# State update of a chunked recurrence: decay of both directions on GpSimd, one addition per head on VectorE

## Chip, cores and metric

One core of a Trainium2 chip runs the kernel. The metric is the device time of one launch in microseconds (us), as the median of the runs shown. Inputs and outputs are float32. TensorE is the matmul engine (PE), VectorE is DVE, ScalarE is ACT, GpSimd is POOL, SyncE is SP, which issues most of the DMAs.

## What is computed

One layer of a hybrid network on 1024 tokens of 2048 features and 256 context tokens: an adaptive layer norm, the input projection `w_in`, three branches (an S5 state space, a pooling branch and an RWKV recurrence), the output projection `w_out`, and a layer norm. The change concerns the RWKV branch: 16 heads of 64, two directions, started from the final states of the context. Its reference, token by token:

```python
def _rwkv_scan(s0, r, w, k, v, kk, kka, reverse, want_out):
    def step(s, inp):
        w_t, k_t, v_t, kk_t, kka_t = inp[:5]
        s_kk = jnp.einsum('bhvk,bhk->bhv', s, kk_t)
        s = (s * w_t[:, :, None, :] - s_kk[..., None] * kka_t[:, :, None, :]
             + v_t[..., None] * k_t[:, :, None, :])
        if want_out:
            return s, jnp.einsum('bhvk,bhk->bhv', s, inp[5])
        return s, None
```

The state `s` of a head is 64x64; it fades by `w_t` per feature and gains outer products.

## The kernel before

The first half (phases A and B, up to about 1700 us) does the layer norm, the input projection and the S5 and pooling branches. Phase C runs the recurrence in chunks of 64 tokens. Two heads make a pair, so there are eight pairs; both directions of a pair go side by side. A pair has four quarters of four chunks, 16 steps in all, and before them four steps over the context (`prefixes`), which only build the starting state. That makes 128 steps and 32 prefix steps.

A step (`c_first`, `c_second`, `c_third`) is a chain. On TensorE, L2009 multiplies the state of each direction with the queries, and L2014 adds the chunk's own part. ScalarE copies the result (`rhs`, L2018). L2024 applies the solved 64x64 system, ScalarE copies (`uv`, L2028), L2037 forms what the state gains, in the bank `b_u`, and L2043 completes the outputs, which ScalarE copies out (`outs`, L2056). Then VectorE updates the state (L2050; L2119 in the prefix): one `scalar_tensor_tensor` per direction and head, state times the chunk's decay `el`, plus the gain from PSUM. In the last step of a pair there is no update. The state lies in `ping`, a 128x128 tile per direction with the two heads as blocks on the diagonal.

Beside the chain other jobs run. `seg_job` loads keys, spreads them into tiles with zero blocks (`spread`, L236 and L234), multiplies (L1745) and masks (L1750). `solve` inverts the small triangles on VectorE (`tmp` and `nn`, L1880 and L1882). `jit_jobs` scale the queries on GpSimd (`qt`, L1843). `finish` normalizes a pair's outputs, in part on GpSimd (`gof`, `gvn`, `gs`), and stores them to `y`. `out_first` takes 12 of the 16 row blocks of the projection `w_out` ahead of time: it loads pieces, gates and splits them into a high and a low half (L240, L234, L236), multiplies three times (L2434 to L2436) and adds to a partial sum in DRAM (`ofev`, L2451 and L2453, then `part`).

The order on every engine is written by a planner, `Pace`. It keeps a clock of its own for each engine; a job yields `need(engine, cost, due times)`. After each third of a step, `fill` lets the planner put other jobs' work into the queues until TensorE's planned time reaches the time when the chain can go on:

```python
        def fill(ch, third=False):
            t = max(ch.t_s[0], ch.t_s[1] - 0.22, ch.t_o) if third else ch.t
            P.offer(max(P.free["pe"] + QUOTA, t + SLACK))
```

So the price that a step's code names decides how much other work stands between two steps. Engines then run their queues strictly in this order.

When the last pair's last quarter begins, the pool of keys (`st`) is closed and `Late.begin` takes its room for the last four blocks of `w_out` (`dwraw`, `dgate`, `dwhi`, `dwlo`, L2503 to L2526). Phase D multiplies these with the last outputs (L2623 to L2625), adds the partial sums (`pre`, loaded from `part`, L2641) and does the final layer norm. `dacc` has four banks, each freed by its addition L2641.

## Time and profile before

| what | value |
|---|---|
| median of 3 runs | 3001.09 us (2996.73 to 3008.69) |
| the profiled execution | 3004.46 us, span 3002.7 us |
| mean granted TensorE clock | 0.928 of full speed |
| PE busy | 2703.1 us (90%) |
| DVE busy | 2017.4 us (67%) |
| ACT busy | 1053.1 us (35%) |
| POOL busy | 1058.8 us (35%) |
| phase C, from the first keys to the last step | about 1700 to 2845 us |
| state update, L2050 and L2119 | 608 instructions, 134.2 + 35.8 us |

The profile tells of one execution. Shares over the whole span mix stages: the input projection until 1650 us is a dense run of large matmuls, while phase C is what the change touches. So a reader goes from the table of stages to the waits in a stage, and from there to single steps in order of time. An instruction's idle time in front of it, with what ended it, stands in square brackets in the timeline.

### The profile page before, as it was taken

Reading aid. Unit: us, or ns where it says so; the run is one execution under the profiler, and the core shown is the slowest. Engines: PE = TensorE matmul, PEld = TensorE weight load, DVE = VectorE, ACT = ScalarE, POOL = GpSimd, SP = SyncE. Lnnn points to the kernel's source line nnn. Section 1 sums busy time; section 2 is a strip of 40 time slices with the busy share of each in tenths; the row PEclk is TensorE's granted clock in tenths of the full one; section 3 lists DMA queues with packets and bytes.
Section 4 is the critical chain, followed back from the end, with each engine's and each line's share of the span. In section 5 each row is a group of like instructions: output and inputs, shape, how many; then the busy total and the mean of one; then the engine's idle time right before and its main releaser. Section 6 shows DMA issues by size and latency. Waiting matters only on the chain. (4 is left out here: it accounts for less than half of the span.)

```text
span 3002.7 us, 56320 instructions
## 1 busy us (share of the span) xinstructions
PE 2703.1 (90%) x20080; PEld 2194.4 (73%) x20080; DVE 2017.4 (67%) x4463; ACT 1053.1 (35%) x2668; POOL 1058.8 (35%) x1432
## 2 busy tenths in 40 slices
PE   7989999999999999999899669988988889898776
PEld 2258878888888887777777467877878778787555
DVE  5548136655666657888888375768778777876458
ACT  1321224444444443222122223343434334443313
POOL 0104003333343334223552133454444434444316
PEclk9989999999999999999999778999979889898688
DMA  7834646667666665555344665676675756564354
GB/s 272 262 109 139 152 123 169 168 170 190 175 171 179 168 174 156 158 161 165 106 116 124 198 192 145 189 186 166 166 190 169 203 146 188 149 182 123 83 199 158
DMA packets 698673, 498.48 MB, mean 166 GB/s; under 512 B 347182, under 2 KB 624406, under 8 KB 695574
## 3 DMA queue, kind: packets, MB, share of 16 engines
q1 hardware_dynamic: 672632, 449.52, 53.8%
q0 software_dynamic: 6912, 24.12, 2.9%
q10 hardware_dynamic: 18848, 21.24, 2.0%
q8 instruction: 159, 2.61, 0.4%
q14 instruction: 122, 1.00, 0.1%
HBM read 339.64 MB, written 155.07 MB: 165 GB/s over the span
## 5 line engine op out<-in xcount | busy, mean ns | idle before, releaser
L300 PE MATMUL pm<-hi,whi 128*128 128x512 f32 x1600 | 512.2, 402 | 4.4 <-ACT whi L300 4.3
L300 PE MATMUL pm<-hi,wlo 128*128 128x512 f32 x1600 | 509.4, 400 | 3.8 <-DVE wlo L300 3.8
L300 PE MATMUL pm<-lo,whi 128*128 128x512 f32 x1600 | 510.0, 400 | 0.0
L300 DVE TENSOR_TENSOR wlo<-wraw,whi 128x256 fp32r<-128x256 f32 x400 | 227.8, 576 | 317.6 <-ACT whi L300 297.8
L300 PEld LDWEIGHTS pm<-hi,whi 128*128 128x128 f32 x1600 | 275.3, 190 | 58.3 <-ACT whi L300 6.2
L300 PEld LDWEIGHTS pm<-hi,wlo 128*128 128x128 f32 x1600 | 275.5, 190 | 55.6 <-DVE wlo L300 5.8
L300 PEld LDWEIGHTS pm<-lo,whi 128*128 128x128 f32 x1600 | 274.5, 190 | 51.1 <-issue 2.2
L300 ACT ACTIVATE whi<-wraw 128x256 fp32r<-128x256 f32 x400 | 160.8, 415 | 415.6 <-DMA wraw<-in_w_in 241.3
L2434 PE MATMUL ofacc<-ofhi,ofyh 128*128 128x256 f32 x768 | 252.1, 328 | 25.9 <-DVE ofev L2451 16.0
L240 POOL TENSOR_TENSOR oflo<-ofw,ofhi 128x256 fp32r<-128x256 f32 x158 | 119.9, 759 | 342.0 <-ACT ofhi L234 226.2
L2435 PE MATMUL ofacc<-ofhi,ofyl 128*128 128x256 f32 x768 | 226.7, 295 | 1.0 <-POOL ofyl L240 1.0
L2436 PE MATMUL ofacc<-oflo,ofyh 128*128 128x256 f32 x768 | 226.4, 295 | 1.2 <-POOL oflo L240 0.9
L1745 PE MATMUL gp<-spread,kq 128*128 128x128 f32 x1152 | 184.7, 312 | 27.9 <-ACT spread L234 12.8
L2050 DVE SCALAR_TENSOR_TENSOR ping<-ping,els,banku 64x64 f32<-64x64 f32 x480 | 134.2, 280 | 111.6 <-PE banku L2037 57.1
L1745 PEld LDWEIGHTS gp<-spread,kq 128*128 128x128 f32 x1152 | 161.6, 217 | 38.0 <-DVE spread L236 12.6
L2434 PEld LDWEIGHTS ofacc<-ofhi,ofyh 128*128 128x128 f32 x768 | 155.5, 203 | 40.2 <-ACT ofhi L234 10.7
L1882 DVE TENSOR_TENSOR nn<-nn,tmp 128x31 f32<-128x31 f32 (+15 forms) x310 | 153.9, 496 | 10.7
L2435 PEld LDWEIGHTS ofacc<-ofhi,ofyl 128*128 128x128 f32 x768 | 156.9, 204 | 1.3 <-POOL ofyl L240 1.2
L2436 PEld LDWEIGHTS ofacc<-oflo,ofyh 128*128 128x128 f32 x768 | 156.4, 204 | 1.8 <-POOL oflo L240 1.3
L1880 DVE TENSOR_TENSOR tmp<-af,nn 128x31 f32<-128x31 f32 (+15 forms) x310 | 146.1, 471 | 13.1 <-DMA af<-flat 4.1
L2009 PE MATMUL banky<-ping,qt 128*128 128x128 f32 x512 | 105.8, 326 | 45.2 <-DVE ping L2050 27.1
L240 POOL TENSOR_TENSOR ofw<-ofw,ofg 128x256 f32<-128x256 f32 x163 | 129.9, 798 | 39.7 <-DMA ofw<-in_w_out 39.6
(512 smaller groups left out, 5496.8 us busy)
## 6 DMA issues: line engine op xcount, KB each, us to landing
wraw<-in_w_in SPq DMA_DIRECT2D x400, 128.0 KB, 2.8
kq<-z_kq SPq DMA_DIRECT2D x80, 512.0 KB, 5.4
araw<-in_w_ada SPq DMA_DIRECT2D x128, 256.0 KB, 3.7
ofw<-in_w_out SPq DMA_DIRECT2D x192, 128.0 KB, 3.4
part<-ofev SPq DMA_DIRECT2D x96, 256.0 KB, 2.7
cds<-z_cd POOLq DMA_DIRECT2D x40, 512.0 KB, 5.2
z_kq<-kq SPq DMA_DIRECT2D x80, 256.0 KB, 3.1
z_kq<-kq SPq DMA_DIRECT2D x160, 128.0 KB, 3.1
```

The costliest lines, as they stand in the source:

```text
L240: (nc.vector if eng == "dve" else nc.gpsimd).tensor_tensor(out, a, b, op=op)
L300: r = x(*args, **kw)
L1745: nc.tensor.matmul(gp[:, i], seg.kb[:, i, :], qb[:, i].rearrange("p h t -> p (h t)"), start=True, stop=True)
L1880: nc.vector.tensor_tensor(tv, af[:, q, q + 1:].unsqueeze(2).to_broadcast([128, nt_, nj]), nn[:, q:q + 1, 0:nj].to_broadcast([128, nt_, nj] ...
L1882: nc.vector.tensor_tensor(nn[:, q + 1:, 0:nj], nn[:, q + 1:, 0:nj], tv, op=OP.subtract)
L2009: nc.tensor.matmul(b_y[:, ch.y + d], seg.qt[:, ch.c[d]], ch.s[d], start=(d == 0), stop=False, skip_group_check=True)
L2050: nc.vector.scalar_tensor_tensor(ch.s[d][hs, hs], ch.s[d][hs, hs], seg.el[hs, ch.c[d]:ch.c[d] + 1], b_u[hs, 2 + d, hs], op0=OP.mult, op1=O ...
L2434: nc.tensor.matmul(o, yh[:, sl], whi, start=(first and b == 0), stop=False, skip_group_check=True)
L2435: nc.tensor.matmul(o, yl[:, sl], whi, start=False, stop=False, skip_group_check=True)
L2436: nc.tensor.matmul(o, yh[:, sl], wlo, start=False, stop=last, skip_group_check=True)
```

## The change

The two states of a pair (one per direction) move into one tile `ping` of 128x2x128. A step's update is split. `fade`, on GpSimd, multiplies the diagonal blocks of both directions with their decays into a small tile `faded`, two instructions of 64x128, one per head; it is put into the queue in `c_first`, right when the state is known. `advance`, on VectorE, adds `faded` and the gain in PSUM, two instructions of 64x2x64, one per head. The prefix steps do the same. The planner's prices for a step's update go from 0.58 us per direction to 0.75 us on GpSimd and 0.42 us on VectorE. Two buffers change beside it: the `spread` tiles lie in the pool `st`, and the first `Late.add` has two `dgate` tiles in place of one.

```diff
-        ping = [[cc.tile([128, 128], FT, name=f"ping{d}{j}") for j in range(2)] for d in range(2)]
+        ping = [cc.tile([128, 2, 128], FT, name=f"ping{j}") for j in range(2)]
+        faded = [cc.tile([128, 2, 64], FT, name=f"faded{j}") for j in range(2)]
...
-        spread = [cc.tile([128, 4, 2, 64], FT, name=f"spread{j}") for j in range(SPREADS)]
+        spread = [st.tile([128, 4, 2, 64], FT, name=f"spread{j}", bufs=1) for j in range(SPREADS)]
...
+        def fade(s, segs, cs, to, *deps):
+
+            i, j = (4 * seg.src + c for seg, c in zip(segs, cs))
+            el = els.rearrange("p s c -> p (s c)")[:, i:j + 1:j - i].unsqueeze(2)
+            for hs in hcs:
+                nc.gpsimd.tensor_tensor(to[hs], s[hs, :, hs], el[hs].to_broadcast([64, 2, 64]), op=OP.mult)
+            return P.run("pool", FADE, *deps)
+
+        def advance(s, of, bank, *deps):
+            for hs in hcs:
+                nc.vector.tensor_tensor(s[hs, :, hs], of[hs], bank[hs, 2:4, hs], op=OP.add)
+            return P.run("dve", GROW, *deps)
+
+        FADE, GROW = 0.75, 0.42
...
+            if go:
+                ch.t_f = fade(ch.s, segs, ch.c, faded[0], ch.t_s)
...
-                for d, seg in enumerate(segs):
-                    for h in range(2):
-                        hs = slice(64 * h, 64 * h + 64)
-                        nc.vector.scalar_tensor_tensor(ch.s[d][hs, hs], ch.s[d][hs, hs], seg.el[hs, ch.c[d]:ch.c[d] + 1],
-                                                       b_u[hs, 2 + d, hs], op0=OP.mult, op1=OP.add)
-                    ch.t_s[d] = P.run("dve", 0.58, max(t))
+                ch.t_s = advance(ch.s, faded[0], b_u, max(t), ch.t_f)
...
-            t = max(ch.t_s[0], ch.t_s[1] - 0.22, ch.t_o) if third else ch.t
+            t = max(ch.t_s, ch.t_o) if third else ch.t
...
-                       for nm, m in (("dgate", num - 1), ("dwraw", num)))
+                       for nm, m in (("dgate", 2), ("dwraw", num)))
```

In the order of instructions the change shows in three places. The first is VectorE at one step of a middle pair, between pieces of the solver. Before:

```order
L1882 TENSOR_TENSOR nn<-nn,tmp 128x13x19
L2050 SCALAR_TENSOR_TENSOR ping_15851<-ping_15851,els,banku 64x64 x2
L2050 SCALAR_TENSOR_TENSOR ping_15853<-ping_15853,els,banku 64x64 x2
L1880 TENSOR_TENSOR tmp<-af,nn 128x240
L1882 TENSOR_TENSOR nn<-nn,tmp 128x12x20
```

With the change, at another step (here a prefix step's update stands beside it; `misc` is the prefix's bank):

```order
L1882 TENSOR_TENSOR nn<-nn,tmp 128x12x20
L2005 TENSOR_TENSOR ping_15850<-faded_15852,banku 64x2x64 x2
L2005 TENSOR_TENSOR ping_15851<-faded_15853,misc_15795 64x2x64 x2
L236 COPY kbnc<-misc_15794 128x512
L1880 TENSOR_TENSOR tmp<-af,nn 128x231
```

Four instructions of a step have become two, and they need what GpSimd wrote into `faded`.

The second place is GpSimd in the last quarters, where the decays now stand among the gating (`ofw`) and splitting (`oflo`) of `w_out`:

```order
L240 TENSOR_TENSOR ofw_15803<-ofw_15803,ofg_15818 128x256
L2000 TENSOR_TENSOR faded_15852<-ping_15851,els 64x128 x2
L240 TENSOR_TENSOR oflo_15811<-ofw_15803,ofhi_15810 128x256
L240 TENSOR_TENSOR ofw_15804<-ofw_15804,ofg_15818 128x256
L240 TENSOR_TENSOR oflo_15807<-ofw_15804,ofhi_15806 128x256
L240 TENSOR_TENSOR ofw_15805<-ofw_15805,ofg_15818 128x256
L2000 TENSOR_TENSOR faded_15852<-ping_15851,els 64x128 x2
```

In the order before, this queue held no work of the chain; 82 of the 152 decays stand right behind an instruction of L240.

The third place is TensorE in the last pair. Before, its steps follow each other with nothing between (`banky`, `banku` are the step's banks):

```order
L2009 MATMUL banky<-ping_15851,qt 128x128
L2009 MATMUL banky<-ping_15853,qt 128x128
L2014 MATMUL banky<-uv_15870,aq 64x64 x4
L2024 MATMUL banku<-rhs,aq 64x64 x4
L2037 MATMUL banku<-uv_15870,kbn 64x64 x4
L2043 MATMUL banky<-uv_15870,ar 64x64 x4
```

With the change, products of `w_out` (`ofacc`, now L2441 to L2443) stand there:

```order
L2040 MATMUL banku<-rhs,aq 64x64 x4
L1827 MATMUL misc_15794<-ident,kq 128x128 x4
L2441 MATMUL ofacc_15815<-ofhi_15810,ofyh_15819 128x256
L2442 MATMUL ofacc_15815<-ofhi_15810,ofyl_15820 128x256
L2443 MATMUL ofacc_15815<-oflo_15811,ofyh_15819 128x256
```

Of the 2304 product matmuls, 78 stood behind the first step of the last pair, and none behind its last step; now 414 stand within the last pair and 180 behind its last step, mixed with the matmuls of phase D.

## Rows read from the trace of the kernel before

**Rows 1.** Table of stages: window, length, busy PE, PEld, DVE, ACT, POOL, clock, DMA.

```profile
1840.00:2757.00 917.00, 813.03 (x10222) 716.14 (x10222) 686.25 (x1762) 369.46 (x1029) 408.10 (x651) 0.90 0.63 172
2757.00:2845.00 88.00, 64.50 (x748) 50.99 (x748) 35.87 (x138) 29.74 (x90) 27.82 (x67) 0.66 0.27 70
2845.00:2880.00 35.00, 12.23 (x35) 7.38 (x32) 13.48 (x35) 6.86 (x14) 13.37 (x27) 0.59 0.84 274
```

**Rows 2.** Waits of PE, 1840 to 2757 us: total us, times, longest.

```profile
PE banky L2009 <- DVE ping L2050: 25.6, 16, 4.2
...
PE banky L2009 <- ACT outs L2056: 7.9, 10, 2.3
```

**Rows 3.** Timeline of DVE near the end: start, duration, in brackets idle before.

```profile
2819.16 1.22 DVE L2050 SCALAR_TENSOR_TENSOR ping<-ping,els,banku 64x64 f32<-64x64 f32 x4 [1.80 <-ACT uv L2028]
2823.50 1.22 DVE L2050 SCALAR_TENSOR_TENSOR ping<-ping,els,banku 64x64 f32<-64x64 f32 x4 [3.12 <-ACT gob L2222]
```

**Rows 4.** Timeline of PE at the same step; the chain of waits (start, duration) earlier.

```profile
2824.30 0.96 PE L2009 MATMUL banky<-ping,qt 128*128 128x128 f32 x4 [0.67 <-ACT outs L2056]
...
1885.71 1.09 PE gp L1745 x8
```

**Rows 5.** Instructions that touch ping: count, ns min/median/max, first and last start.

```profile
L2050 DVE SCALAR_TENSOR_TENSOR ping<-ping,els,banku x480: 261/280/290, 1845.8 to 2840.9; 64x64 f32<-64x64 f32 x160
```

**Rows 6.** Timeline of DVE, and a group of DVE by line (busy us, mean ns).

```profile
2314.21 0.28 DVE L1880 TENSOR_TENSOR tmp<-af,nn 128x135 f32<-128x135 f32 x1
...
L2451 DVE TENSOR_TENSOR ofev<-ofacc,ofev 128x512 f32<-128x512 f32 x64 | 43.2, 686 | 16.3 <-PE ofacc L2436 7.7 <-DMA ofev<-part 7.5
```

**Rows 7.** Solver on DVE beside POOL, timeline; its groups on the page.

```profile
2307.53 0.39 DVE L1882 TENSOR_TENSOR nn<-nn,tmp 128x220 f32<-128x220 f32 x1
2307.78 0.74 POOL L240 TENSOR_TENSOR oflo<-ofw,ofhi 128x256 fp32r<-128x256 f32 x1 [0.53 <-ACT ofhi L234]
2307.95 0.80 DVE L1880 TENSOR_TENSOR tmp<-af,nn 128x207 f32<-128x207 f32 x1
...
2316.05 0.22 DVE L1880 TENSOR_TENSOR tmp<-af,nn 128x60 f32<-128x60 f32 x1
...
L1882 DVE TENSOR_TENSOR nn<-nn,tmp 128x31 f32<-128x31 f32 (+15 forms) x310 | 153.9, 496 | 10.7
...
L1880 DVE TENSOR_TENSOR tmp<-af,nn 128x31 f32<-128x31 f32 (+15 forms) x310 | 146.1, 471 | 13.1 <-DMA af<-flat 4.1
```

**Rows 8.** Groups of POOL by line and shape, 1700 to 2850 us.

```profile
L2238 POOL TENSOR_TENSOR gof<-gof,gs 128x256 f32<-128x256 f32 x29 | 18.5, 639 | 0.1
...
L2202 POOL TENSOR_TENSOR gs<-gs 128x8 f32<-128x8 f32 x45 | 9.9, 220 | 45.5 <-DVE gs L2198 43.2
```

**Rows 9.** Timeline of PE: products at full clock, then at the lower one.

```profile
2306.08 0.28 PE L2434 MATMUL ofacc<-ofhi,ofyh 128*128 128x256 f32 x1
2306.20 0.28 PE L2435 MATMUL ofacc<-ofhi,ofyl 128*128 128x256 f32 x1
...
2315.37 0.41 PE L2435 MATMUL ofacc<-ofhi,ofyl 128*128 128x256 f32 x1
2315.58 0.41 PE L2436 MATMUL ofacc<-oflo,ofyh 128*128 128x256 f32 x1
```

**Rows 10.** DMA issues: count, KB each, median us to landing.

```profile
part<-ofev SPq DMA_DIRECT2D x96, 256.0 KB, 2.7
...
pre<-part SPq DMA_DIRECT2D x8, 1024.0 KB, 9.4
```

**Rows 11.** Waits of PE, 2757 to 3003 us.

```profile
PE dacc L2623 <- ACT yhi L2588: 19.6, 3, 10.2
...
PE dacc L2623 <- ACT dwhi L2523: 3.4, 2, 2.1
```

**Rows 12.** Timeline of POOL at the start of phase C.

```profile
1701.38 1.04 POOL L1843 TENSOR_TENSOR qtc<-kq,els 128x512 f32<-128x512 f32 x1 [53.08 <-DMA kq<-z_kq]
```

**Rows 13.** Waits of POOL, 1840 to 2757 us.

```profile
POOL oflo L240 <- ACT ofhi L234: 208.3, 89, 11.7
```

More of the change, by code (lines that the diff above doesn't have):

```diff
@@ L2008, in c_first @@
             for d, seg in enumerate(segs):
-                nc.tensor.matmul(b_y[:, ch.y + d], seg.qt[:, ch.c[d]], ch.s[d], start=(d == 0), stop=False,
+                nc.tensor.matmul(b_y[:, ch.y + d], seg.qt[:, ch.c[d]], ch.s[:, d], start=(d == 0), stop=False,
                                  skip_group_check=True)
-                P.run("pe", 0.22, ch.t_s[d], ch.t_o, seg.t_made)
+                P.run("pe", 0.22, ch.t_s, ch.t_o, seg.t_made)
             for d, seg in enumerate(segs):
@@ L2072, in prefixes @@
                 if pr.pair > 1:
-                    for t in pr.s:
-                        for h in range(2):
-                            nc.gpsimd.memset(t[64 * h:64 * h + 64, 64 * h:64 * h + 64], 0.0)
-                    pr.t_s = [P.run("pool", 0.4)] * 2
+                    for hs in hcs:
+                        nc.gpsimd.memset(pr.s[hs, :, hs], 0.0)
+                    pr.t_s = P.run("pool", 0.4)
                 uv = wk.tile([128, 8, 128], FT, name="uvc", tag="uvc", bufs=1)
@@ L2085, in prefixes @@
                     for d, seg in enumerate(segs):
-                        nc.tensor.matmul(bank[:, d], seg.qt[:, cs[d]], pr.s[d], start=(d == 0), stop=False,
+                        nc.tensor.matmul(bank[:, d], seg.qt[:, cs[d]], pr.s[:, d], start=(d == 0), stop=False,
                                          skip_group_check=True)
@@ L2093, in prefixes @@
                     t = P.run("pe", 0.24, t_in, t, tile=64)
+                    yield need("pool", FADE, pr.t_s)
+                    t_f = fade(pr.s, segs, cs, faded[1], pr.t_s)
                     yield need("act", 0.27, t)
@@ L2114, in prefixes @@
                     t = P.run("pe", 0.24, t, tile=96)
-                    yield need("dve", 1.16, t)
-                    for d, seg in enumerate(segs):
-                        for h in range(2):
-                            hs = slice(64 * h, 64 * h + 64)
-                            nc.vector.scalar_tensor_tensor(pr.s[d][hs, hs], pr.s[d][hs, hs], seg.el[hs, cs[d]:cs[d] + 1],
-                                                           bank[hs, 2 + d, hs], op0=OP.mult, op1=OP.add)
-                        pr.t_s[d] = P.run("dve", 0.58, t)
-                    misc.give(i, pr.t_s[1])
+                    yield need("dve", GROW, t, t_f)
+                    pr.t_s = advance(pr.s, faded[1], bank, t, t_f)
+                    misc.give(i, pr.t_s)
                 release(segs)
@@ L2292, in phase_c @@
             pr.uv, pr.t_uv = [None] * 2, [0.0] * 2
-            pr.s, pr.t_s = [ping[d][n % 2] for d in range(2)], [0.0, 0.0]
+            pr.s, pr.t_s = ping[n % 2], 0.0
             pairs.append(pr)
```

14 lines of the change are left out of this document (6 added, 8 removed).

## The prediction, made before the change was timed

> **What bounds the kernel now.** I read the table of stages first. In the recurrence of pairs 0 to 6 (1840 to 2757 us) TensorE is busy 813 of 917 us at a granted clock of 0.90, VectorE 686, GpSimd 408 [rows 1]: TensorE leads. Then the stage changes: in the last pair (2757 to 2845 us) TensorE is busy 64.5 of 88 us at 0.66, and in the 35 us behind it only 12.2 [rows 1]. The products of w_out (L2434 to L2436) are what fills TensorE during pairs 0 to 6, and by the order before only 78 of their 2304 matmuls are left for the last pair and none for the time behind it. So the same chip waits twice: first the recurrence behind the products, then TensorE with nothing to do.
>
> Next, who keeps TensorE waiting in pairs 0 to 6: the state update 25.6 us in 16 waits, the output copies 7.9 in 10 [rows 2]. So about 26 of some 105 steps wait at their first matmul; in the others TensorE comes late itself.
>
> Last, one bare step. Near the end, with no product between, the updates start 4.34 us apart [rows 3]. The state matmuls take 0.96 us there, and what releases the first is the output copy on ScalarE (0.67 us), not the update [rows 4]; the second stands until the second direction's update is done. Four such passes at full clock take half of the 1.09 us of eight, 0.54 [rows 4].
>
> **The change, part by part.** *VectorE's update.* Removed: 480 + 128 instructions of 0.28 us [rows 5], 170 us. Added: 120 + 32 steps with two additions of 64x128, one input in PSUM. A two-input instruction of 128x135 took 0.28 us [rows 6]. With a PSUM input, 512 columns took 686 ns [rows 6], hence a quarter of it, 0.17, is the lower end; the upper is 0.39, what 220 columns took alone [rows 7]. I take 0.28, the nearest size. 304 x 0.28 = 85 us, so VectorE is freed of 85 us. On a step's path an update falls from 1.22 [rows 3] to about 0.58, but the gain is smaller: both state matmuls now start together behind both additions, or behind the output copy. What is left of the 0.96 is 0.54, so a bare step gains 0.42 us.
>
> *GpSimd's decay.* Added: 304 multiplications of 64x128. 256 columns took 639 ns, 8 columns 220 [rows 8]: a line between them gives 0.42 us for 128, which I take; the ends are 0.22 and 0.64. A step needs 0.84 us, all of it 128 us. It runs beside the step: from one update's end to the next start are 4.34 - 1.22 = 3.1 us, so 2.3 us of slack cover it. Without that cover it would cost 0.84 in every step.
>
> *The planner.* Here lies the large term. A step's fill used to aim at 0.94 us behind the update's start (the later of 0.58 and 1.16 - 0.22), now at 0.42: 0.52 us less product work per step, some 67 us in 128 steps. The order confirms the size: behind the first step of the last pair now stand 414 products within the pair and 180 after the last step, instead of 78 and 0. So 516 matmuls leave pairs 0 to 6. Products follow each other at 0.12 us at full clock and at 0.21 at the lower one [rows 9]; at 0.90 that is 0.133, and 516 of them are 69 us. Where TensorE leads, the stretch shortens by that much: **-69**. The lower end is 25.6, if only the waits for the state go; the upper 77, if the stretch keeps its ratio of full-clock work to time (0.90 x 813/917 = 0.80) and 516 x 0.12 us are divided by it.
>
> *The last pair.* It takes 336 more products, 40 us at full clock. Its own work is 64.5 x 0.66 = 43; 83 us at the ratio of 0.80 last 104 us instead of 88: **+16**. If the clock stays low, at 0.21 per product and no gap used, it is 71; if all slip into gaps, 0.
>
> *Behind the last step.* 180 products are 22 us at full clock, 27 at 0.80. The hole of 35 us has 23 free [rows 1], so 4 stand over. The last rows of partial sums now come later as well: addition 0.69 [rows 6], store 2.7 us, load 9.4 [rows 10], 13 us until the first sum of block 4 can free its bank. By the order, 18 products and then the matmuls of block 4's second unit come last there, which want that bank: nothing covers these 13. Together **+17**. Lower end 0, since the stage waits anyway for the last pair's rows (19.6 us [rows 11]); upper end 40, when of the 27 nothing is hidden.
>
> *Plan against chip.* The plan takes 0.52 us off a step, a bare step gains 0.42. The 0.10 left over is at most 12 us in 120 steps if each waits for its state; about a quarter waits now, more will with less fill. I take **+6**; ends 0 and 12.
>
> *Contention.* nn of 220 columns took 0.39 us alone; tmp of 207 took 0.80 beside a GpSimd multiplication [rows 7]. By 0.39 at 220 and 0.22 at 60 columns, the 620 instructions of the solver (20 runs of 31, 5456 columns each) would take 213 us alone; they took 146.1 + 153.9 = 300 [rows 7]. So 87 us went beside GpSimd, mostly beside its 408 us in pairs 0 to 6 [rows 1], 0.21 per us: 128 us of decay cost VectorE about 27 more. Against 85 freed I take 0 on the path; ends -25.6 (no wait for the state left) and +27. The Trainium skill, "GPSIMD Engine Reference", sections Specifications and Engine selection, speaks against this change: elementwise work on two inputs belongs on VectorE, GpSimd being about twice as slow, and GpSimd shares its SBUF interfaces with VectorE, in contention with instructions that have two SBUF inputs. The trace agrees: 0.39 against 0.80 us. By that rule I would add the 27 us and take off nothing for the relief.
>
> *Small edits.* Half of the 24 clearing memsets go: 0, GpSimd is 45% busy. The spread tiles lie in another pool, so their two memsets now stand behind the release of that pool, as the first qtc did; that one sat 53.08 us until its keys landed [rows 12], and this covers them; uncovered they would cost about the 1.04 us of that instruction. The second gate buffer spares SyncE a wait before a load; TensorE waits only 3.4 us for the pieces behind it [rows 11]: 0 to -3.4, I take 0. GpSimd's queue gains a wait: a decay stands until the state before it is done, and behind it the splits of w_out stand, for which products wait on TensorE; the slack above covers it on plan.
>
> **Sum.** -69 + 16 + 17 + 6 = -30 us. Against the profiled execution's 3004.5 us (span 3002.7) that is 2974.5; the median of the runs is 3.4 us lower, so I predict **2971 us**.
>
> **The rivals.** (a) *The work only changes its place.* If waits for DMAs and the solver hold the recurrence and not the products, pairs 0 to 6 lose only 25.6 us; with 16 + 17 + 6 the sum is +13, 3014 us. For it: those other waits stay as they are; against it: 813 of 917 us busy.
>
> (b) *Decay comes late.* GpSimd works in order. In pairs 0 to 6 it sat 208.3 us in 89 waits for ScalarE's ofhi [rows 13], 2.3 us each. Harmless then; now 82 of 152 decays stand right behind an instruction of L240, nearly all of them splits of w_out. If 152 updates are late by 0.55 us on average beyond the slack of 2.3 us, 84 us come on top: 3055 us. It decides from 0.30 us per step on (45 us), where the result passes 3016. Against it: those waits are long because nothing presses GpSimd, and the planner counts the decays.
>
> (c) *Contention falls on the solver.* If all of its 27 us lie on the path and the relief gives nothing: 2998 us. The rule of the Trainium skill named above would have it so; the trace shows the price, not the place.
>
> **How the numbers follow.** Forecast 0.65, (a) 0.17, (b) 0.13, (c) 0.05. About 0.5% (15 us) is what a measurement of this kernel can tell from no change: faster means under 2986, slower over 3016. (a) and (c) lie within: faster 0.65, same 0.22, slower 0.13. The forecast's own ends: with the upper value of the first term (-77), no loss behind the last step nor from the plan, and +16, the sum is -61, 2940; with half of the 25.6 us of waits for the state gone as well, 2927. I put the low end at 2925. The high end, 3015, takes in (a) and (c) and leaves out (b).
>
> **What would show it.** Right: the last product of w_out lies behind the last step; the last pair takes 95 to 110 us at a clock near 0.9; pairs 0 to 6 end some 60 to 75 us earlier; the additions last about 0.28 us, the decays 0.42; few waits of VectorE's addition for GpSimd. Wrong: additions that wait for decays over 50 us in total (b); the first pairs as long as before, with TensorE idle (a); tmp and nn longer than 320 us in sum (c); or a stage behind the last step that grows by more than 40 us, as the late products hold it up.

## The result, and the profile after

The changed kernel takes **2966.33 us** (median of 4 runs, 2957.10 to 2971.75), the kernel before 2998.91 beside it (4 runs): a ratio of 0.9886, 95% interval 0.9846 to 0.9925. It is faster, by 1.1%, and 5 us below the predicted 2971. The profiled execution took 2957.1 us (span 2955.3), 9 us less than its median, and that of before 5.6 us more than its own: the two traces lie 47 us apart where the medians lie 33 apart. So single terms are read from the traces, as one execution each, and verdicts from the timed ratios.

The table of stages, before and then after, cut at the first state matmul of the first step, of the last pair and of the last step (L2009 before, L2023 after). Columns as in [rows 1].

```profile
1834.83:2755.13 920.30, 812.00 (x10214) 715.11 (x10212) 687.79 (x1766) 368.36 (x1028) 409.98 (x653) 0.90 0.63 173
2755.13:2840.63 85.50, 62.99 (x736) 49.74 (x732) 33.34 (x134) 29.47 (x88) 25.02 (x55) 0.66 0.28 71
2840.63:3002.70 162.07, 107.88 (x428) 82.08 (x428) 114.48 (x191) 42.72 (x74) 69.55 (x74) 0.81 0.53 175
```

```profile
1832.58:2669.30 836.72, 725.03 (x9658) 633.00 (x9659) 612.13 (x1503) 344.81 (x962) 462.60 (x846) 0.93 0.62 168
2669.30:2762.40 93.10, 88.38 (x1071) 78.97 (x1071) 56.96 (x156) 31.12 (x93) 58.18 (x104) 0.96 0.68 198
2762.40:2955.30 192.90, 127.34 (x610) 102.68 (x608) 134.57 (x222) 45.77 (x80) 74.71 (x79) 0.85 0.54 178
```

Pairs 0 to 6 lose 83.6 us, the last pair gains 7.6, the stage from the last step on gains 30.8, and what lies ahead of the recurrence is 2.3 shorter (it takes 1822 to 1835 us in the profiles of this document, so this difference says nothing): together -47.4. By the order, 1968 product matmuls stood between the first step and the last pair, and now 1470; 0 stood within the last pair, and now 342; 0 behind the start of the last step, and now 180. The other 24 of these 522 stood ahead of the first step. (The prediction's counts of 78 and 414 take in those that stand in the gap just ahead of the last pair's first step: 78 then, 72 now.)

TensorE's waits in pairs 0 to 6 (total us, times, longest), which answer to [rows 2]:

```profile
PE banky L2023 <- DVE ping L2005: 46.4, 30, 3.4
...
PE gp L1745 <- DVE spread L236: 8.7, 12, 1.7
```

The state is waited for more often than before (30 waits in place of 16), since with less fill TensorE comes back to the chain early. TensorE's idle time in all hardly moved: 920.3 - 812.0 = 108 us before, 836.7 - 725.0 = 112 after. What fell is its busy time.

The instructions that touch the state (count, ns min/median/max, first and last start), which answer to [rows 5], and then the decay's group on the page (busy us, mean ns, idle before):

```profile
L2000 POOL TENSOR_TENSOR faded<-ping,els x304: 391/400/667, 1803.0 to 2759.2; 64x128 f32<-64x128 f32 x152
L2005 DVE TENSOR_TENSOR ping<-faded,banku x240: 269/286/294, 1841.4 to 2761.8; 64x128 f32<-64x128 f32 x120
L2005 DVE TENSOR_TENSOR ping<-faded,misc x64: 266/286/294, 1812.5 to 2611.8; 64x128 f32<-64x128 f32 x64
```

```profile
L2000 POOL TENSOR_TENSOR faded<-ping,els 64x128 f32<-64x128 f32 x304 | 127.2, 419 | 138.4 <-DVE ping L2005 125.9
```

The two prices that the trace of before did not show came out as taken: 286 ns for an addition (0.28), 419 ns for a decay (0.42). Now the waits of VectorE for a decay, 1800 to 2770 us, and of GpSimd, 1840 to 2680 us, which answer to [rows 13]:

```profile
DVE ping L2005 <- POOL faded L2000: 1.0, 1, 1.0
```

```profile
POOL faded L2000 <- DVE ping L2005: 120.6, 67, 5.8
POOL oflo L240 <- ACT ofhi L234: 58.2, 31, 4.3
```

One addition out of 152 pairs waited for its decay, for 1 us. It is GpSimd that waits, at the chain's state, and its old waits for ScalarE's halves have shrunk from 208 us to 58. The solver's groups on the page, which answer to [rows 7]:

```profile
L1880 DVE TENSOR_TENSOR tmp<-af,nn 128x31 f32<-128x31 f32 (+15 forms) x310 | 147.4, 476 | 22.4 <-DMA af<-flat 13.4
L1882 DVE TENSOR_TENSOR nn<-nn,tmp 128x31 f32<-128x31 f32 (+15 forms) x310 | 153.8, 496 | 10.9 <-DMA uvc<-z_v 0.2
```

Their sum is 301.2 us against 300.0. Last, the stage from the last step on. Before, TensorE waited 19.6 us for `yhi` [rows 11], and besides for the low half `ylo`, mostly of a later row block (first fence); the second fence shows its waits after.

```profile
PE dacc L2624 <- DVE ylo L240: 5.7, 2, 5.5
```

```profile
PE dacc L2631 <- DVE ylo L240: 18.3, 2, 14.8
PE dacc L2630 <- ACT yhi L2595: 10.6, 2, 5.8
PE dacc L2630 <- DVE pre L2648: 10.1, 1, 10.1
PE ofacc L2441 <- DVE ofev L2458: 6.2, 5, 4.1
```

And the timeline of the wait for `pre`, on VectorE, SyncE and TensorE in turn (start, duration, in brackets idle before):

```profile
2829.61 1.41 DVE L2458 TENSOR_TENSOR ofev<-ofacc,ofev 128x512 f32<-128x512 f32 x2 [0.50 <-PE ofacc L2443]
...
2839.66 0.69 DVE L2648 TENSOR_TENSOR pre<-dacc,pre 128x512 f32<-128x512 f32 x1 [3.38 <-DMA pre<-part]
```

```profile
2831.57 0.39 SPq L2463 DMA_DIRECT2D part<-ofev  x1
2832.66 0.86 SPq L2610 DMA_DIRECT2D pre<-part  x2
```

```profile
2840.41 0.80 PE L2630 MATMUL dacc<-dwhi,yhi 128*128 128x512 f32 x1 [10.12 <-DVE pre L2648]
```

This is the chain that the prediction named: the last partial sum is added, stored, loaded again, and only its sum frees a bank of `dacc`. TensorE stands 10.12 us for it.

### The profile page after: what moved, and what is told of

Read it like the earlier page. It is cut to its first block, busy times and chain, and to the rows that moved or that the text cites. A ratio compares the mean times of both kernels' runs of the same rounds, so it can differ in the third digit from the quotient of the medians.

```text
span 2955.3 us, 56419 instructions
## 1 busy us (share of the span) xinstructions
PE 2653.7 (90%) x20080; PEld 2156.8 (73%) x20080; DVE 1985.1 (67%) x4247; ACT 1032.9 (35%) x2611; POOL 1149.9 (39%) x1681
## 5 line engine op out<-in xcount | busy, mean ns | idle before, releaser
L2441 PE MATMUL ofacc<-ofhi,ofyh 128*128 128x256 f32 x768 | 250.1, 326 | 22.6 <-DVE ofev L2458 10.8
L2443 PE MATMUL ofacc<-oflo,ofyh 128*128 128x256 f32 x768 | 224.8, 293 | 3.0 <-POOL oflo L240 3.0
L1745 PE MATMUL gp<-spread,kq 128*128 128x128 f32 x1152 | 177.2, 303 | 30.5 <-ACT spread L234 12.8
L240 POOL TENSOR_TENSOR oflo<-ofw,ofhi 128x256 fp32r<-128x256 f32 x147 | 111.9, 761 | 203.2 <-ACT ofhi L234 78.0
L1745 PEld LDWEIGHTS gp<-spread,kq 128*128 128x128 f32 x1152 | 153.8, 209 | 41.5 <-DVE spread L236 12.5
L2441 PEld LDWEIGHTS ofacc<-ofhi,ofyh 128*128 128x128 f32 x768 | 153.5, 200 | 39.5 <-DVE ofev L2458 12.7
L2000 POOL TENSOR_TENSOR faded<-ping,els 64x128 f32<-64x128 f32 x304 | 127.2, 419 | 138.4 <-DVE ping L2005 125.9
L2443 PEld LDWEIGHTS ofacc<-oflo,ofyh 128*128 128x128 f32 x768 | 154.4, 201 | 3.5 <-POOL oflo L240 3.5
L240 POOL TENSOR_TENSOR ofw<-ofw,ofg 128x256 f32<-128x256 f32 x143 | 115.1, 807 | 43.2 <-DMA ofw<-in_w_out 42.1
L2023 PE MATMUL banky<-ping,qt 128*128 128x128 f32 x512 | 86.9, 294 | 48.2 <-DVE ping L2005 46.4
```

The costliest lines, as they stand in the source:

```text
L240: (nc.vector if eng == "dve" else nc.gpsimd).tensor_tensor(out, a, b, op=op)
L1745: nc.tensor.matmul(gp[:, i], seg.kb[:, i, :], qb[:, i].rearrange("p h t -> p (h t)"), start=True, stop=True)
L2000: nc.gpsimd.tensor_tensor(to[hs], s[hs, :, hs], el[hs].to_broadcast([64, 2, 64]), op=OP.mult)
L2023: nc.tensor.matmul(b_y[:, ch.y + d], seg.qt[:, ch.c[d]], ch.s[:, d], start=(d == 0), stop=False, skip_group_check=True)
L2441: nc.tensor.matmul(o, yh[:, sl], whi, start=(first and b == 0), stop=False, skip_group_check=True)
L2443: nc.tensor.matmul(o, yh[:, sl], wlo, start=False, stop=last, skip_group_check=True)
```

## The experiments

The theory was the prediction's: products move out of the stretch where TensorE leads, and that is the gain; the instructions themselves (GpSimd's decay, the shorter update) change nothing on the path. Three rivals: the instructions gain as well, through a VectorE with less to do; GpSimd's decay costs, through contention; and a change of the plan of any size moves the time at random.

All runs in one table. Stages are from one profile each (us), counts from the order, ratios from the timed runs, each to the kernel before timed beside it.

| run | ratio (95%) | pairs 0-6 | last pair | from last step | products 0-6, last pair, behind |
|---|---|---|---|---|---|
| before | 1 | 920.3 | 85.5 | 162.1 | 1968, 0, 0 |
| after | 0.9886 (0.9846-0.9925) | 836.7 | 93.1 | 192.9 | 1470, 342, 180 |
| old instructions, lower price | 0.9901 (0.9884-0.9918) | 877.8 | 96.2 | 162.1 | 1644, 348, 0 |
| old instructions, price 0.56 | 0.9966 (0.9949-0.9983) | 907.4 | 86.7 | 162.7 | 1920, 48, 0 |
| new instructions, old aim | 0.9862 (0.9845-0.9879) | 871.3 | 88.2 | 162.2 | 1884, 96, 0 |
| after's order, old instructions | 0.9953 (0.9935-0.9971) | 856.8 | 96.0 | 194.4 | as after |
| after's order, decay on VectorE | 0.9980 (0.9964-0.9996) | 875.5 | 95.1 | 193.0 | as after |
| decay on VectorE, planned so | 0.9960 (0.9947-0.9972) | 891.4 | 96.7 | 163.4 | 1662, 312, 0 |
| decay twice | 0.9941 (0.9922-0.9959) | 852.3 | 97.3 | 192.3 | as after |
| last pair filled more | 0.9874 (0.9849-0.9899) | 839.5 | 118.9 | 172.3 | 1470, 426, 96 |
| one gate buffer, as before | 0.9900 (0.9878-0.9921) | 845.7 | 96.7 | 200.4 | as after |
| prices 0.75 and 0.82 | 0.9849 (0.9825-0.9872) | 870.3 | 93.3 | 162.7 | 1824, 156, 0 |
| prices 0.75 and 0.66 | 0.9864 (0.9839-0.9889) | 866.1 | 95.9 | 164.8 | 1710, 282, 0 |
| prices 0.84 and 0.66 | 0.9791 (0.9769-0.9814) | 848.9 | 97.5 | 162.8 | 1638, 354, 0 |

How far one profile of a stage can be trusted, two of these runs show: the one with one gate buffer and the one with the last pair filled more have, through pairs 0 to 6, the change's instructions in the change's order. These are their pairs 0 to 6, in this order:

```profile
1831.81:2677.49 845.68, 736.26 (x9658) 643.55 (x9659) 609.61 (x1503) 344.20 (x962) 460.69 (x846) 0.91 0.62 166
1827.03:2666.53 839.50, 732.31 (x9659) 639.14 (x9659) 612.17 (x1504) 344.91 (x962) 462.36 (x846) 0.92 0.62 167
```

With the change's own 836.7 us at 0.93 that is three executions of the same work, 9 us apart, and their granted clocks differ as well. In pairs 0 to 6, differences of that size between two profiles are not read as effects below.

**Old instructions, lower price.** The kernel before with only the planner's price changed; no instruction is another.

```diff
-                    ch.t_s[d] = P.run("dve", 0.58, max(t))
+                    ch.t_s[d] = P.run("dve", 0.32, max(t))
...
-                    yield need("dve", 1.16, t)
+                    yield need("dve", 0.64, t)
...
-                        pr.t_s[d] = P.run("dve", 0.58, t)
+                        pr.t_s[d] = P.run("dve", 0.32, t)
```

> The kernel before, with one edit: the planner's price of a state update is 0.32 us per direction in place of 0.58, so that a step's fill aims at 0.42 us behind the update's start, as in the change; every instruction stays as before. By the order 522 product matmuls then leave the part up to the last pair's first step, all into the last pair (348), none behind the last step. Theory (the gain is the moved fill): pairs 0 to 6 lose up to 69 us, give back up to 0.52 us per step in new waits for the state (at most 55 us in 105 steps, I expect half, 28), the last pair grows by some 16, so about 25 us faster than before, near 2975. Rival (the new instructions bring the gain, the plan only follows): no gain without them, 3000, or slower by the 0.52 us per step, up to 3050.

Measured: 2960.30 us against 2991.72, -1.0%. The expectation's 522 does not fit its own 348: the order has 348 in the last pair, 324 of them out of pairs 0 to 6 and 24 from ahead. At the prediction's 0.133 us each, 324 are 43 us, and the stretch is 42.5 shorter. The waits for the state, which were to give back 28 us, grew from 25.6 to 30.2 only. Nothing stands behind the last step, and that stage stays at 162. So moving products alone gains, at about the price that the prediction put on it.

**New instructions, old aim.** The changed kernel, with the price of the addition raised so that the fill aims at about 0.94 us again:

```diff
-        FADE, GROW = 0.75, 0.42
+        FADE, GROW = 0.75, 0.94
```

> The changed kernel, with one edit: the planner's price of the addition is 0.94 us in place of 0.42, so that a step's fill aims where it did before; decays on GpSimd and additions on VectorE stay. By the order the products mostly stay in the first seven pairs (96 within the last one, none behind it). Theory (moved fill): only the waits for the state go (25.6 us at most in pairs 0 to 6), plus 0.42 us in some 15 bare steps: 10 to 30 us faster than before, 2970 to 2990; less than the whole change by some 10 to 20 us. Rival (the instructions): the whole gain stays, about 33 us, 2966.

Measured: 2950.78 us, -1.4%, the theory's number missed. Only 84 products left pairs 0 to 6 (11 us at 0.133), yet they are 49 us shorter. So some 38 us come from the instructions by the traces, and some 33 by the timed ratio (41 us, less the 11, with the last pair's 2.7 added). The theory's "nothing on the path" falls here for the first time. Below, in the change's own order, the same instructions bring 20; why this order gains more from them was not tried.

**Decay on VectorE, planned so.** `fade` on VectorE, with a price to match:

```diff
-                nc.gpsimd.tensor_tensor(to[hs], s[hs, :, hs], el[hs].to_broadcast([64, 2, 64]), op=OP.mult)
-            return P.run("pool", FADE, *deps)
+                nc.vector.tensor_tensor(to[hs], s[hs, :, hs], el[hs].to_broadcast([64, 2, 64]), op=OP.mult)
+            return P.run("dve", FADE, *deps)
...
-        FADE, GROW = 0.75, 0.42
+        FADE, GROW = 0.58, 0.42
```

(and the same in the prefix's `need`).

> The changed kernel with the decay (the two multiplications of a step) on VectorE in place of GpSimd, at a planned price of 0.58 us; still ahead of time, still one addition per head. GpSimd then has no work of the chain, and its 127 us of decay no longer stand beside the solver. Theory: what counts is that the decay lies off the chain, not where it runs; VectorE gets 304 x 0.28 = 85 us back, and saves up to 27 us of contention; no product lies behind the last step. Within 15 us of the changed kernel, about 2966. Rival (VectorE's relief of 85 us is the gain): about 3000, as before.

Measured: 2980.99 us, -0.4%, some 22 us slower than the change: neither the theory's 15 at most nor the rival's "as before". With 306 products moved (41 us) the pairs are only 29 us shorter, beside a VectorE as full as before. TensorE's wait for VectorE's `spread` is 25.5 us in 20 waits here and 8.7 in 12 in the change; but the fastest kernel below waits 24.6 us for it as well, so across orders this wait does not tell fast from slow. The two runs in one order, further down, do.

**Decay twice.** Every decay is issued a second time, with the same result:

```diff
-            for hs in hcs:
+            for hs in hcs + hcs:
```

> The changed kernel with each decay computed twice (four multiplications per step, the same result), the planned order unchanged. A decay then takes 1.7 us of a step's 3.1 us of room. Theory (the decay is covered): 0 to 15 us slower than the changed kernel, by contention with VectorE at 0.21 us per us of GpSimd (27 us of VectorE's time at most); few waits of the addition for the decay. Rival (GpSimd sits on the chain): 0.84 us in each of 128 steps, up to 107 us slower, 3070.

Measured: 2972.90 us, 0.9941 where the change has 0.9886, 16 us slower by these ratios; the intervals just touch. GpSimd does 110 us more in pairs 0 to 6 (572.6 against 462.6). The wait for a decay and the solver's groups in this run:

```profile
DVE ping L2005 <- POOL faded L2000: 1.1, 2, 0.6
```

```profile
L1880 DVE TENSOR_TENSOR tmp<-af,nn 128x31 f32<-128x31 f32 (+15 forms) x310 | 150.8, 487 | 20.0 <-DMA af<-flat 11.0
L1882 DVE TENSOR_TENSOR nn<-nn,tmp 128x31 f32<-128x31 f32 (+15 forms) x310 | 156.0, 503 | 10.7
```

Even at twice the length the decays are not late, and tmp and nn grow by 5.6 us to 306.8. Additions that wait for a late decay are ruled out as a cost. What the 16 us are is not shown.

**Old instructions, price 0.56.** A control: the kernel before with a price that moves a few products, 0.56 and 1.12 in place of 0.58 and 1.16.

```diff
-                    ch.t_s[d] = P.run("dve", 0.58, max(t))
+                    ch.t_s[d] = P.run("dve", 0.56, max(t))
...
-                        pr.t_s[d] = P.run("dve", 0.58, t)
+                        pr.t_s[d] = P.run("dve", 0.56, t)
```

> A control: the kernel before with the planned price of a state update at 0.56 us per direction in place of 0.58; no instruction changes, the planner only writes a slightly different order (48 products move into the last pair, none behind it). It shows how much a new order alone scatters the time. Theory (the time follows the moved products and the clock): 48 x 0.133 us, 6 us faster than before, and within 10 us of it. Rival (any new order of this planner can bring 30 us, and the gains of the change and of the first two experiments are scatter): 15 us or more away from before, to either side.

Measured: 2987.52 us against 2994.57. That is 10 us by the ratio (-0.34%) and 7 by the medians, where 48 moved products make 6. So the scatter of this one other plan is a few us; it explains neither the 33 us of the change nor those of the run with the old aim.

**After's order, old instructions.** The changed kernel's order with only the arithmetic taken back: `fade` issues nothing, and `advance` multiplies and adds as before.

```diff
-            for hs in hcs:
-                nc.gpsimd.tensor_tensor(to[hs], s[hs, :, hs], el[hs].to_broadcast([64, 2, 64]), op=OP.mult)
+            decays[id(to)] = segs, cs
...
-            for hs in hcs:
-                nc.vector.tensor_tensor(s[hs, :, hs], of[hs], bank[hs, 2:4, hs], op=OP.add)
+            for d, (seg, c) in enumerate(zip(*decays[id(of)])):
+                for hs in hcs:
+                    nc.vector.scalar_tensor_tensor(s[hs, d, hs], s[hs, d, hs], seg.el[hs, c:c + 1],
+                                                   bank[hs, 2 + d, hs], op0=OP.mult, op1=OP.add)
```

> The changed kernel in its own order, but without its new instructions: no decay on GpSimd, and in place of the two additions the four fused instructions of the kernel before. It has the moved products without the shorter update. If plan and instructions each give their part (42 and 49 us in pairs 0 to 6 by the first two experiments), the part of the instructions is missing: 498 products x 0.133 = 66 us less, 15 to 40 us back in waits for the state, last pair 12 and last stage 31 us longer: between 5 us faster and 20 us slower than before. Rival (the plan alone brings all of it): as the changed kernel, 1.1% faster than before.

**After's order, decay on VectorE.** Again the same order, only the engine of the decay changed:

```diff
-                nc.gpsimd.tensor_tensor(to[hs], s[hs, :, hs], el[hs].to_broadcast([64, 2, 64]), op=OP.mult)
+                nc.vector.tensor_tensor(to[hs], s[hs, :, hs], el[hs].to_broadcast([64, 2, 64]), op=OP.mult)
```

> The changed kernel in exactly its order on TensorE, ScalarE and SyncE, the decays alone given to VectorE, at the place where GpSimd's decay stood (the planner still counts them on GpSimd). VectorE loses the relief of 85 us and is spared the contention of 27. Theory (moved fill; the decay is off the chain wherever it runs): 5 to 15 us slower than the changed kernel. Rival (VectorE's relief is the other half of the gain, as the experiment with the old aim suggests): 25 us or more slower.

These two and the change have all their other instructions in the same order, so they split it cleanly. Measured: old instructions 2982.42 us (-0.47%), decay on VectorE 2989.71 (-0.20%), both slower than the change with its -1.14%, with intervals apart from it. Of the first expectation neither the theory nor the rival holds: the run is some 14 us faster than before, where the theory said 5 at most, and not as fast as the change. The theory had the new waits for the state too large, 15 to 40 us; they grew from 25.6 to 32.9. Of the second, the rival came true: 28 us slower than the change. Pairs 0 to 6 in each, first old instructions, then the decay on VectorE:

```profile
1833.35:2690.15 856.80, 747.41 (x9659) 646.74 (x9660) 662.37 (x1771) 344.66 (x962) 350.92 (x579) 0.92 0.61 164
```

```profile
1821.99:2697.49 875.50, 745.59 (x9659) 651.30 (x9660) 684.40 (x1769) 343.97 (x962) 352.93 (x579) 0.90 0.60 160
```

The order alone makes pairs 0 to 6 63.5 us shorter (920.3 to 856.8). The instructions take another 20 off (856.8 to 836.7; 11 against the slowest of the three profiles of the change's order), and with the decay on VectorE the stretch is 38.8 longer than with it on GpSimd (at least 30). The timed ratios put the whole kernels 20 and 28 us above the change. VectorE is busy 612, 662 and 684 us in the three. Where that shows on TensorE, two groups in each (busy us, mean ns, then idle before): the change, old instructions, decay on VectorE.

```profile
L1745 PE MATMUL gp<-spread,kq 128*128 128x128 f32 x936 | 142.4, 299 | 14.8 <-DVE spread L236 8.7 <-DVE aq L1750 4.0 <-ACT spread L234 2.1
...
L2023 PE MATMUL banky<-ping,qt 128*128 128x128 f32 x448 | 76.3, 295 | 48.2 <-DVE ping L2005 46.4 <-ACT outs L2067 1.3 <-ACT ofhi L234 0.4
```

```profile
L1745 PE MATMUL gp<-spread,kq 128*128 128x128 f32 x936 | 141.2, 297 | 22.7 <-DVE spread L236 16.9 <-DVE aq L1750 4.5 <-ACT af L1888 0.7
...
L2025 PE MATMUL banky<-ping,qt 128*128 128x128 f32 x449 | 89.6, 312 | 37.5 <-DVE ping L2005 32.9 <-ACT outs L2069 2.1 <-ACT ofhi L234 0.3
```

```profile
L1745 PE MATMUL gp<-spread,kq 128*128 128x128 f32 x936 | 149.6, 309 | 30.6 <-DVE spread L236 22.6 <-DVE aq L1750 7.0 <-ACT spread L234 0.4
...
L2023 PE MATMUL banky<-ping,qt 128*128 128x128 f32 x449 | 80.4, 306 | 51.2 <-DVE ping L2005 48.5 <-ACT outs L2067 2.0 <-DVE gs L2197 0.4
```

Busy and idle of the state matmuls together are 124.5, 127.1 and 131.6 us, and 121.2 and 120.8 in the other two profiles of the change's order: the faster update is worth 3 to 6 us against the old one here. The two directions' matmuls no longer wait one behind the other (busy 76.3 against 89.6), but the wait ahead of the first grows. The chunk's key products (`gp`) take 157.2, 163.9 and 180.2; the other two profiles have 165.0 and 162.4, so in this sum only the decay on VectorE stands out. In the wait for VectorE's `spread` both do, with 16.9 and 22.6 us against 8.7 (10.2 and 9.3 in the other two): in one and the same order, a VectorE with more to do brings the keys later. Solver against contention: tmp and nn sum to 279.8 us with the old instructions and 279.5 with the decay on VectorE, but 301.2 in the change (296.5 and 299.3 in the other two). GpSimd's decay does cost VectorE 17 to 21 us there, and the change is the fastest of the three all the same.

**Last pair filled more.** In the last pair the fill may reach further ahead (`LASTQ` 1.6 in place of `QUOTA` where no pair follows):

```diff
-            P.offer(max(P.free["pe"] + QUOTA, t + SLACK))
+            P.offer(max(P.free["pe"] + (QUOTA if ch.more else LASTQ), t + SLACK))
...
-            ch.s, ch.t_s = pr.s, pr.t_s
+            ch.s, ch.t_s, ch.more = pr.s, pr.t_s, after
```

> The changed kernel with a larger quota of fill (1.6 us in place of 0.8) in the last pair only: by the order 426 products stand within the last pair in place of 342, and 96 behind the last step in place of 180; the rest is as in the changed kernel. Theory: the last pair grows by 84 x 0.133 = 11 us, the last stage loses as much of the products, but still waits for its last partial sums: within 8 us of the changed kernel. Rival (what stands behind the last step costs more than its own time): 10 us or more faster than the changed kernel.

Measured: 2961.21 us against 2994.57, 0.9874, as the change and as the theory had it in sum. Its two parts were twice as large: 84 products came forward, the stage behind lost 20.6 us, and the last pair grew by 25.8 where 11 were expected. What is left behind the last step cost about as much as in the pair, which had no gaps left.

**Prices near the truth.** Three kernels with the changed instructions and other prices for decay and addition, to keep the gain without products behind the last step:

```diff
-        FADE, GROW = 0.75, 0.42
+        FADE, GROW = 0.84, 0.66
```

> The changed kernel with planned prices near the measured ones (0.84 us for the decays of a step, 0.66 for the additions with their margin) in place of 0.75 and 0.42. By the order 354 products stand within the last pair and none behind the last step; 1638 stand between the first step and the last pair, against 1470 in the changed kernel and 1968 before. Theory (products moved, plus some 20 us from the instructions, minus the loss behind the last step): pairs 0 to 6 lose 330 x 0.133 = 44 and 20 us, the last pair grows by 10, the last stage stays at 162: 54 us less than before in the sum of the parts, 2940 to 2950. Rival (less moved is less gained): slower than the changed kernel, 2970 or more.

```diff
-        FADE, GROW = 0.75, 0.42
+        FADE, GROW = 0.75, 0.82
```

> The changed kernel with a planned price of 0.82 us for the additions: between the changed kernel and the experiment with the old aim. 156 products within the last pair, none behind the last step. Theory: pairs 0 to 6 lose 144 x 0.133 = 19 and 20 us from the instructions, last pair up to 5 longer, last stage as before: 2955 to 2965. Rival (the version with the old aim was a lucky order): 2970 or more.

```diff
-        FADE, GROW = 0.75, 0.42
+        FADE, GROW = 0.75, 0.66
```

> The changed kernel with a planned price of 0.66 us for the additions, the decays left at 0.75: 282 products within the last pair, none behind the last step, 1710 before the last pair. Theory: 258 x 0.133 = 34 and 20 us less in pairs 0 to 6, the last pair 8 longer: 2945 to 2955. Rival: a new order scatters by 10 us either way, 2940 to 2975.

Measured against 2997.11: 2933.34 us, 2953.44 and 2957.59. The first is 7 us faster than its range, the second 2 faster and the third 3 slower, so the parts add up to within some us, and the third's rival (an order scatters by 10 us) is not out. The first beats both kernels, by 2.1% against before and, with intervals apart, about 1% against the change. Its stages, and TensorE's wait for the state in pairs 0 to 6:

```profile
1830.14:2679.04 848.90, 746.16 (x9854) 654.65 (x9855) 618.75 (x1479) 352.55 (x978) 490.61 (x865) 0.93 0.64 173
2679.04:2776.54 97.50, 93.73 (x1058) 83.91 (x1055) 54.68 (x159) 33.68 (x99) 60.29 (x117) 0.91 0.60 176
2776.54:2939.30 162.76, 104.64 (x430) 79.35 (x428) 113.66 (x192) 43.56 (x75) 67.15 (x67) 0.82 0.53 179
```

```profile
PE banky L2023 <- DVE ping L2005: 26.4, 18, 3.9
```

A decay now costs 0.84 in the plan (two of 419 ns) and an addition 0.66 (two of 286 ns are 0.57). 330 products leave pairs 0 to 6, 354 fill the last pair, and none is left behind: the last stage is back at 162.8. With 0.75 for the decay and the same 0.66 the kernel is 0.7% slower. Its pairs 0 to 6 are 17 us longer, and 72 products more stand in them, which at 0.133 us make 10; the rest is within what one profile can differ by. But the run with 0.82, which moved fewer still, is no slower than it, so the count of products alone does not set the order of the three.

**One gate buffer.** The last small edit taken back:

```diff
-                       for nm, m in (("dgate", 2), ("dwraw", num)))
+                       for nm, m in (("dgate", num - 1), ("dwraw", num)))
```

> The changed kernel with one gate buffer for the first three late blocks, as before the change; the order is the changed kernel's up to the last step. Theory: the second buffer was priced at 0 to 3.4 us: within 4 us of the changed kernel, which no such measurement can tell from none. Rival (the spared wait on SyncE matters, since late products now queue behind it): 8 us or more slower.

Measured: 2966.24 us against 2997.11, 0.9900. No difference from the change in time. Its profile, 10 us above its median, has 200.4 us in the last stage, where the profiles of the same order with two buffers have 192.3 to 194.4; the timed runs show no loss from it. The move of the `spread` tiles to another pool was not taken back in any run.

## Why the prediction was right, and where a step was not

| term | predicted | in the two profiles | what isolates it |
|---|---|---|---|
| products out of pairs 0 to 6 | -69 | part of -83.6 | old instructions in after's order: -63.5 |
| instructions (plan +6, relief and contention 0) | +6 | part of -83.6 | same order, new against old: -11 to -20 |
| last pair | +16 | +7.6 | +10.5 with old instructions |
| behind the last step | +17 | +30.8 | +32 with old instructions |
| small edits | 0 | -2.3 ahead of the recurrence | one gate buffer: no difference; the others not taken back |
| sum | -30 | -47 (medians -33) | |

By the signs named beforehand: the additions, the decays, tmp and nn, the waits for decays and the last stage (under 40 us more) came as said; pairs 0 to 6 ended 85.8 us earlier, 11 more than the upper end of 60 to 75, and the last pair took 2 us less than its band of 95 to 110.

**The large term held.** 498 products fewer at 0.133 us are 66 us (the prediction's 516 take in 24 from ahead of these pairs and leave out 6 of the gap), and the order alone made it 63.5; the lower price with old instructions moved 324 (43 us) and gained 42.5. Part of this closeness is luck, as the profile of before is a slow one. Counted from the control (907.4 us with 1920 products), the same two orders gain 50.6 us for 450 products and 29.6 for 276. So a product moved out was worth 0.11 to 0.13 us. That is what "where TensorE leads, the stretch shortens by that much" said. Rival (a), by which those pairs lose only 25.6 us, is out.

**The step that failed: "Against 85 freed I take 0 on the path".** In the same order the new instructions are 20 us faster than the old by the timed ratios, and 28 faster than with the decay on VectorE; the run with the old aim shows 33 to 38 from the instructions. The +6 beside it, for a plan that asks more of a bare step than it gives, is not seen as a loss either, although the waits for the state grew from 25.6 to 46.4 us. Before, the state matmuls and their idle time took, in pairs 0 to 6:

```profile
L2009 PE MATMUL banky<-ping,qt 128*128 128x128 f32 x448 | 88.1, 315 | 35.5 <-DVE ping L2050 25.6 <-ACT outs L2056 7.9 <-POOL qt L1843 1.0
```

That is 123.6 us together, and now it is 76.3 and 48.2, or 124.5: the second direction's matmuls stopped waiting inside their group, which pays for the longer wait ahead of it. And VectorE was late not only with the state, but also with the keys, `spread`, ahead of `gp`.

**Rival (c), contention.** The 27 us were a little large: 17 to 21 more in tmp and nn with the decay on GpSimd than without it. (The GpSimd instruction that the prediction calls a multiplication in [rows 7] is a split's subtraction, `oflo`.) On the path they did not outweigh the relief. Their sum against before hardly rose (301.2 and 300.0). Other GpSimd work left the stretch, so that it went from 410 to 463 us, +53 and not +128; at 0.21 that would still be 11 us, which the sum does not show. The Trainium skill, "GPSIMD Engine Reference", Specifications and Engine selection, would put this two-input operation on VectorE, as GpSimd is about twice as slow and contends for SBUF. The trace agrees with both statements in part: 419 ns here on GpSimd against a median of 289 on VectorE, and the 17 to 21 us. But the measurement decides against the choice: in the same order, the kernel with the decay on VectorE is about 1% slower (0.9980 against 0.9886), with TensorE's waits for VectorE longer (48.5 and 22.6 us against 46.4 and 8.7).

**Rival (b), late decays.** 1.0 us of waits in all, 1.1 with every decay done twice. The slack of 2.3 us per step held, and GpSimd's waits for ScalarE's halves had room to give: 208 us became 58.

**Last pair, mis-sized: +7.6 for +16.** The sum of work was right (63 us at 0.66 and 342 products at 0.12 are 83 full-clock us), but the prediction kept the ratio of 0.80. With the gaps filled TensorE was granted 0.96, not about 0.9, and was busy 88.4 of 93.1 us.

**Behind the last step, mis-sized: +30.8 for +17.** The term failed in two places. First, the hole. Half of the products did go into it: 90 of the 180 run within 27 us of the last step's start. Yet TensorE's waits for `yhi` fell only from 19.6 to 10.6 us, so the hole gave back 9 us and not 23, since the rows themselves came later. Below are TensorE's two long waits for them before, the same two after, and then the issue of the first rows' load, before and after:

```profile
2858.58 0.80 PE L2623 MATMUL dacc<-dwhi,yhi 128*128 128x512 f32 x1 [8.95 <-ACT yhi L2588]
2873.18 0.79 PE L2623 MATMUL dacc<-dwhi,yhi 128*128 128x512 f32 x1 [10.23 <-ACT yhi L2588]
```

```profile
2789.43 0.79 PE L2630 MATMUL dacc<-dwhi,yhi 128*128 128x512 f32 x1 [5.78 <-ACT yhi L2595]
2800.11 0.80 PE L2630 MATMUL dacc<-dwhi,yhi 128*128 128x512 f32 x1 [4.85 <-ACT yhi L2595]
```

```profile
2852.70 0.43 SPq L2584 DMA_DIRECT2D yraw<-z_y  x1
2783.35 0.50 SPq L2591 DMA_DIRECT2D yraw<-z_y  x1
```

Counted from the start of the last step, the load is issued after 20.9 us instead of 12.0; in SyncE's queue the loads and stores of the late products (`ofw`, `ofev`, `part`) now stand ahead of it. That they cause the delay was not isolated.

Second, the chain with nothing to cover it. It is there, 10.1 us for the 13, but there is another wait that the prediction does not have, for the low half of a later row block:

```profile
2884.37 0.63 ACT L2595 ACTIVATE yhi<-yraw 128x512 fp32r<-128x512 f32 x1 [0.23 <-DMA yraw<-z_y]
2901.18 0.69 DVE L240 TENSOR_TENSOR ylo<-yraw,yhi 128x512 fp32r<-128x512 f32 x1
2901.92 0.79 PE L2631 MATMUL dacc<-dwhi,ylo 128*128 128x512 f32 x1 [14.79 <-DVE ylo L240]
```

ScalarE has the high half done at 2885.0 us; VectorE takes the low half at 2901.2, behind the additions and the normalization of earlier rows in its queue. All five profiles of the order with 180 products behind have both waits (9.5 to 10.5 and 14.8 to 14.9 us). The run with 96 behind has neither, only one of 5.5 for `ylo` as before, and its stage is 10.2 us longer than before's. In sum, TensorE's busy time in the stage rose by 19.5 us and its idle time by 11.4. Two terms came out better than forecast and this one worse; they partly cancel, and the result was nearer than its terms.

**Open.** TensorE's idle time in pairs 0 to 6 is about the same before, after and with the old instructions in after's order (108, 112 and 109 us); the last 20 us show as shorter busy time of the same matmuls, 747 against 725. Part is the state's group (13.3 us less). Part goes with a granted clock of 0.93 against 0.92, and the clock differs as much between executions of the change's own order (0.91, 0.92 and 0.93). Against those two at 0.91 and 0.92, which take 845.7 and 839.5 us, the old instructions at 0.92 are 11 and 17 us longer; that much stays at nearly the same clock. Why the clock differs is open. A kernel that frees VectorE without loading GpSimd, which would price contention on the path by itself, was not tried.

## What to carry to other kernels

Where a planner writes the order, a price in it is part of the kernel: in the stretch where TensorE led, each product moved out was worth 0.11 to 0.13 us, and the same instructions ran about 1% faster with the best of the price settings tried, which is also near the measured durations (a neighbouring setting gained 0.2%, which is not clear of noise, so measure several). Move filler into a last stretch that has gaps, but count what is left behind the last step of the chain: here the holes of that stage hid little of it (+31 us for 180 products, +10 for 96), and the first rows that end them were loaded later as well. And a slower engine may be the better place: weigh its duration and its contention against what the engine that others wait for is late with, by taking the order as given and changing only the engine.

## What was not expected of the hardware

An addition with one input in PSUM took 266 to 294 ns in all 304 cases, while GpSimd was busy more than half of the time; the solver's instructions, with both inputs in SBUF, lost 17 to 21 us of some 300. And contention did not grow in proportion to GpSimd's work: the decays added 17 to 21 us to tmp and nn over the profiles of the change's order, doubling them (110 us more in pairs 0 to 6) only 6 to 10, where the prediction's 0.21 us per us would give 23. The granted clock of the last pair rose from 0.66 to 0.96 when 342 products filled its gaps.
